# One matmul-bias-residual kernel: another order of the last loads and stores on the one DMA queue

## The chip, the cores and the metric

The kernel runs on one core of one Trainium2 chip. The metric is device time in microseconds (us), the median over several executions. Sizes in this text are binary: 1 MB is 1024 KB.

## The reference

```python
def setup_inputs():
    batch, m, k, n = 16, 512, 1024, 768
    ...

def reference(x, weight, bias, residual):
    return (np.matmul(x, weight) + bias + residual).astype(np.float32)
```

All inputs and the output are float32. x is 32 MB, the residual and the output 24 MB each, the weight 3 MB. All of it has to cross between HBM and the core once: 83 MB.

## The kernel before

**Tiling.** The 8192 rows of x are cut into eight groups of 1024 rows. Partition p of a group holds eight consecutive rows, so each partition's share of a group is one contiguous piece: 32 KB of x, 24 KB of residual, 24 KB of output. A group's x is 4 MB (`x0` to `x7`), its residual 3 MB (`r0` to `r7`), its output 3 MB (`st0` to `st7`). A letter behind the number is a part of a group: `x6a` and `x6b` are the two halves of x of group 6 (2 MB each, `PARTS`), `st7a`, `st7b` and `st7c` are three, three and two of the eight rows (`LAST_PARTS`). `st4+` is one transfer for the outputs of groups 4 and 5. `st7a` is cut further by `shares`: one transfer of partitions 16 to 127 and four of four partitions each.

**Stages.** For each half group (four row tiles of 128 rows) ScalarE casts x to bf16 (L131), VectorE transposes 32-by-32 blocks (L161 and L167), ScalarE moves blocks into place (L136), TensorE multiplies with the weight that stays in SBUF (L326), VectorE adds the residual to the product in PSUM and writes the sum over the residual in SBUF (L173), GpSimd adds the bias in place (L222, two row tiles an instruction, 32 instructions in all). The sum is then stored from the residual's place. VectorE works on half 0 of a group, then on the last four tiles of the group before it (two instructions at L173), then on half 1, then on the first four tiles of the same group. Ahead of these last it waits for the group's residual (`res.wait()` in half 1).

**Places in SBUF.** x alternates between two slots (`x_home`): group g's x can only be loaded when group g - 2 has been cast. The residuals alternate between four slots (`r_home`): the residual of group g from 4 to 6 can only be loaded when the output of group g - 4 has been stored from that slot. Group 7's residual goes into the x slot of group 6.

**Order of the transfers.** All transfers are issued by SyncE onto one DMA queue, in the order written out in `ORDER` (L17). The queue takes them one after another. In the loop at L248 SyncE meets the following waits, and a wait holds back all that is behind it in `ORDER`:

- an x of group g over 1 waits until all four casts of group g - 2 are done (L259), and until the x load before it has landed, because they count on one semaphore (`load_into`, L245, recorded at L87); the second halves (`b`) count on another;
- a residual waits until the residual before it has landed (the same L245), and in groups 4 to 6 until `st{g-4}` has landed (L274);
- the residual of group 7 waits until all casts of group 6 are done (L270); just behind that wait SyncE also releases half 1 of group 7 to ScalarE, since x7 is loaded whole (L272);
- a store waits until GpSimd has added the bias to its last tiles (L285), the last part until VectorE has written it (L283).

The lines that give the waits of the steps below:

```python
258            if g > 1 and part != "b":
259                wait(sp, "cast", 2 * (2 * g - 2))
...
269            if g == n_grp - 1:
270                wait(sp, "cast", 2 * (2 * g))
...
273            elif g > 3:
274                wait(sp, f"st{g - 4}", 16)
```

At L262 a program counts which x groups are loaded whole, so that ScalarE's wait for their second half is met.

Of the kernel before, what the change touches and what calls it, by code (L numbers as in the profile page):

```python
# [14 lines left out]
B = 4  # L15

ORDER = ("x0a bias w x0b r0 x1a x1b r1 x2 r2 x3 r3 x4 st0 "  # L17
         "st1 r4 x5 r5 st2 x6a x6b r6 x7 r7 st3 st4+ st6 st7a st7b st7c").split()
PARTS = {"": (0, 8), "a": (0, 4), "b": (4, 8)}
LAST_PARTS = {"a": (0, 3), "b": (3, 6), "c": (6, 8)}  # L20
SPLIT = "st7a"
# [342 lines left out]
```

## Time and profile before

| | us |
|---|---|
| median of 3 runs | 209.06 (208.9 to 209.13) |
| the profiled execution's own time | 209.15 |
| its span, first to last instruction | 207.4 |
| TensorE matmul busy | 170.5 (82%) |
| VectorE busy | 166.4 (80%) |
| ScalarE busy | 144.9 (70%) |
| GpSimd busy | 115.4 (56%) |
| packets on the 16 DMA engines | 98.2% of the span, 87.05 million bytes, 420 GB/s |

The span leaves out what lies before the first and behind the last instruction of the program: 209.15 - 207.4 = 1.8 us. The median, not the profiled execution, is the time that a change is compared with; the two are 0.09 us apart. A transfer has two times: its issue, when SyncE hands it to the queue, and its landing, when its semaphore is complete. The landing can be read off where SyncE waits for it: the next instruction starts some 0.05 us later.

### The profile page before, as it was taken

To read this page: it belongs to the slowest core of one execution; us is meant where nothing else is said; L and a number is where in the kernel's file an instruction comes from. 1 tells how busy PE (TensorE), PEld (TensorE's weight loads), DVE (VectorE), ACT (ScalarE), POOL (GpSimd) and SP (SyncE) were. 2 spreads that over 40 slices of the span, in tenths; PEclk is the share of its full clock that TensorE was granted. 3 is DMA by queue.
4 is the path that set the end of the run, shared out by engine and by line. 5 is a ranking of instruction groups with operands and counts; after the bars stand their busy time and mean duration, and the time that the engine had idled before them with its cause. 6 is when DMAs were issued, how large, how long until landed. Compare 5 with 4: busy or idle time off the path is not lost.

```text
span 207.4 us, 2314 instructions
## 1 busy us (share of the span) xinstructions
PE 170.5 (82%) x1024; PEld 50.6 (24%) x512; DVE 166.4 (80%) x180; ACT 144.9 (70%) x162; POOL 115.4 (56%) x38
## 2 busy tenths in 40 slices
PE   0000799999999999999999999899999999999900
PEld 0000123322222233323332333233323332222200
DVE  1185493999899998999899988998999899983510
ACT  2393966697879796979697879888797969730000
POOL 0009006609392939385856666484829391999800
PEclk9999999999999999999999999999999999999995
DMA  6999999999999999999999999999999999999995
GB/s 205 448 427 438 431 430 417 450 441 461 405 405 461 398 455 405 438 422 455 441 403 465 411 450 398 422 442 452 403 460 411 450 403 431 455 427 422 436 404 212
DMA packets 4328, 87.05 MB, mean 420 GB/s; under 512 B 484, under 2 KB 484, under 8 KB 616
## 3 DMA queue, kind: packets, MB, share of 16 engines
q1 hardware_dynamic: 4328, 87.05, 98.2%
HBM read 61.88 MB, written 25.17 MB: 420 GB/s over the span
## 4 chain that ended last, share of the span: by engine, by line
DMA 77%; PE 10%; DVE 4%; issue 2%; ACT 1%; SPq 0%; DVEq 0%; ACTq 0%
DMA data<-in_x_dram 66%; DMA out_dram<-data 12%; PE po L326 10%; DVE xt L167 2%; DVE data L173 1%; ACT xb L131 1%; DVE tq L161 1%; SPq L294 0%; DVEq L98 0%; SPq L87 0%; ACTq L98 0%; SPq L359 0%; SPq L45 0%
## 5 line engine op out<-in xcount | busy, mean ns | idle before, releaser
L326 PE MATMUL po<-w_sb,xt 128*128 128x512 bf16 (+1 forms) x1024 | 170.5, 329 | 26.1 <-issue 22.2
L222 POOL TENSOR_TENSOR data<-data,bias_bc 128x1536 f32<-128x1536 f32 x32 | 109.8, 3449 | 65.8 <-DVE data L173 65.7
L136 ACT COPY xt<-tq 32x512 uint32<-32x512 uint32 x128 | 78.9, 617 | 21.8 <-DVE tq L161 19.0
L167 DVE STREAM_TRANSPOSE xt<-xb 32x512 uint32<-32x512 uint32 x128 | 90.1, 704 | 3.9 <-ACT xb L131 2.0
L326 PEld LDWEIGHTS po<-w_sb,xt 128*128 x512 | 50.6, 99 | 145.6 <-issue 143.7
L131 ACT CAST xb<-data 128x2048 bf16 x32 | 64.8, 2076 | 15.7 <-DMA data<-in_x_dram 15.4
L173 DVE TENSOR_TENSOR data<-po,data 128x1536 f32 (+2 forms) x33 | 55.9, 1709 | 13.9 <-PE po L326 13.5
L161 DVE STREAM_TRANSPOSE tq<-xb 128x1024 uint32<-128x1024 uint32 x16 | 19.8, 1236 | 5.5 <-ACT xb L131 5.5
L217 POOL CAST w_sb<-data 128x3072 bf16<-128x3072 f32 x2 | 5.4, 2744 | 15.2 <-DMA data<-in_weight_dram 15.2
L178 DVE LOAD_MASK_SELECT bias_bc<-bias_rows x1 | 0.0, 14 | 6.6 <-DMA bias_rows<-in_bias_dram 6.6
L140 ACT ACT_TABLE_LOAD x1 | 1.3, 1283 | 1.0 <-SPq L45 1.0
L175 DVE MEMSET bias_rows<- 128x768 f32 x1 | 0.7, 698 | 1.2 <-SPq L45 1.2
L178 DVE STREAM_SHUFFLE bias_bc<-bias_rows 128x768 f32<-128x768 f32 x1 | 1.0, 1029 | 0.0
L348 POOL MEMSET const-float32-0.0<- 128x1 f32 x1 | 0.1, 99 | 0.2 <-issue 0.2
L140 ACT COPY warm<-const-float32-0.0 128x1 f32<-128x1 f32 x1 | 0.2, 191 | 0.0
L348 POOL MEMSET const-bfloat16-1.0<- 128x1 bf16 x1 | 0.1, 102 | 0.0
L348 POOL MEMSET const-uint8-127<- 128x1 uint8 x1 | 0.1, 102 | 0.0
L348 POOL MEMSET const-float32-1.0<- 128x1 f32 x1 | 0.1, 99 | 0.0
## 6 DMA issues: line engine op xcount, KB each, us to landing
data<-in_residual_dram SPq DMA_DIRECT2D x8, 3072.0 KB, 17.0
data<-in_x_dram SPq DMA_DIRECT2D x5, 4096.0 KB, 21.8
out_dram<-data SPq DMA_DIRECT2D x5, 3072.0 KB, 24.1
data<-in_x_dram SPq DMA_DIRECT2D x6, 2048.0 KB, 18.5
out_dram<-data SPq DMA_DIRECT2D x1, 6144.0 KB
data<-in_weight_dram SPq DMA_DIRECT2D x1, 3072.0 KB, 13.0
out_dram<-data SPq DMA_DIRECT2D x1, 1152.0 KB
out_dram<-data SPq DMA_DIRECT2D x1, 1008.0 KB
```

The lines of the kernel that those rows point to most:

```text
L131: act.copy(out=xb[:, c], in_=part.rearrange("p t (a j r) -> p t j a r", j=R // 2, r=2)).then_inc(sem("cast"), 1)
L136: act.copy(out=xt[q * Q:(q + 1) * Q, half, :, :, m * Q:(m + 1) * Q], in_=tq[m * Q:(m + 1) * Q, :, :, q]).then_inc(sem("mv"), 1)
L140: act.copy(out=warm[:], in_=nc.const_aps.tensor(0.0, [P, 1], FP32))
L161: dve.transpose(out=tq[:], in_=xb_words(0)).then_inc(sem("tq"), 1)
L167: ins = dve.transpose(out=xt[q * Q:(q + 1) * Q, half, :, :, m * Q:(m + 1) * Q], in_=words[m * Q:(m + 1) * Q])
L173: dve.tensor_add(out=rt, in0=po[:, j % 4:j % 4 + n, :N], in1=rt).then_inc(sem("ev"), 1)
L175: dve.memset(bias_rows[:], 0.0).then_inc(sem("ev"), EV0)
L178: dve.stream_shuffle(out=bias_bc[:], in_=bias_rows[:], mask=[0] * 32).then_inc(sem("bb"), 1)
L217: pool.tensor_copy(out=w_sb[:, part, :], in_=w_stage[:, part, :]).then_inc(sem("wc"), 1)
L222: pool.tensor_add(out=rt, in0=rt, in1=bias_bc[:, None, :].to_broadcast((P, 2, N))).then_inc(sem("add"), 1)
L326: ins = pe.add_instruction(mybir.InstMatmult(name=nc.get_next_instruction_name(), ins=[pe.lower_ap(w_sb[:, k, n0:n0 + nl]), stationary(i, k)],
L348: nc = _bacc.Bacc("TRN2", target_bir_lowering=False, num_devices=1)
```

## The change

Only the string `ORDER` is changed:

```diff
 ORDER = ("x0a bias w x0b r0 x1a x1b r1 x2 r2 x3 r3 x4 st0 "
-         "st1 r4 x5 r5 st2 x6a x6b r6 x7 r7 st3 st4+ st6 st7a st7b st7c").split()
+         "st1 r4 x5 r5 x6 st2 x7 r6 st3 r7 st4+ st6 st7a st7b st7c").split()
```

x of group 6 becomes one transfer of 4 MB in place of two of 2 MB, and stands ahead of `st2`. x of group 7 stands ahead of the residual of group 6. `st3` stands between the residuals of groups 6 and 7, no longer behind both. Through L262 group 6 now counts among the groups that are loaded whole. The instructions of all engines but SyncE are the same in number and order; SyncE issues one transfer less. The bytes are the same.

## The prediction

> **What bounds the kernel now.** I read the DMA queue's row first, then the chain of waits for the landings, then the stretches between landings, then the engines around the two groups whose transfers move.
>
> The queue's row on the page:
>
> ```profile
> q1 hardware_dynamic: 4328, 87.05, 98.2%
> ```
>
> The 16 DMA engines are occupied for 98.2% of the span. The chain of waits (start, duration, what) and, behind it, the stretches between those landings (length, busy time and instructions of each engine, clock, DMA share, GB/s):
>
> ```profile
> 54.62 17.00 DMA data<-in_x_dram
> ...
> 72.06 23.97 DMA out_dram<-data
> ...
> 96.48 24.12 DMA data<-in_x_dram
> ...
> 120.66 19.69 DMA data<-in_x_dram
> ...
> 140.41 21.87 DMA data<-in_x_dram
> ```
>
> ```profile
> 54.60:71.62 17.02, 16.53 (x102) 4.90 (x50) 16.18 (x17) 14.12 (x14) 10.86 (x4) 1.00 1.00 431
> 96.03:120.60 24.57, 24.08 (x149) 7.22 (x74) 23.59 (x26) 19.00 (x22) 13.70 (x4) 1.00 1.01 435
> 120.60:140.35 19.75, 18.75 (x116) 5.58 (x57) 18.33 (x22) 17.75 (x20) 13.73 (x4) 1.00 0.99 424
> 140.35:162.28 21.93, 21.44 (x133) 6.43 (x66) 20.98 (x23) 18.12 (x21) 13.73 (x4) 1.00 1.02 439
> 162.28:196.00 33.72, 33.23 (x205) 9.91 (x102) 27.01 (x27) 18.00 (x20) 26.68 (x8) 1.00 1.00 431
> 204.90:206.10 1.20, 0.00 (x0) 0.00 (x0) 0.00 (x0) 0.00 (x0) 0.00 (x0) 0.50 0.23 97
> ```
>
> Each piece of the chain ends with a landing: x3 at 71.62, st0 at 96.03, x5 at 120.60, x6a at 140.35, x7 at 162.28. Between them the DMA share is 0.99 to 1.02, so the reader is to see a queue that never runs dry. The pace follows: r2 and x3, 7 MB, take 17.02 us, 2.43 us a MB; x6b, r6 and x7, 9 MB, take 21.93, again 2.44. I use 2.434. At that pace the 18 MB behind x7 (r7, st3, st4+, st6, st7) would end at 162.28 + 43.81 = 206.1; SyncE's last wait, for the stores, ends at 206.5. So the kernel is a stream of 83 MB, fed without gaps from the first load to the last store. In the last 1.2 us only a quarter of the DMA time is used: the four small transfers of st7a leave four of the 16 engines with more rows, and these end last.
>
> **The change part by part.** SyncE's issues around it, before:
>
> ```profile
> 110.96 0.33 SPq L294 DMA_DIRECT2D data<-in_residual_dram  x1
> 111.34 0.42 SPq L294 DMA_DIRECT2D out_dram<-data  x1
> 120.66 0.80 SPq L294 DMA_DIRECT2D data<-in_x_dram  x2
> 135.49 0.33 SPq L294 DMA_DIRECT2D data<-in_residual_dram  x1
> 140.41 0.33 SPq L294 DMA_DIRECT2D data<-in_x_dram  x1
> 155.76 0.33 SPq L294 DMA_DIRECT2D data<-in_residual_dram  x1
> 156.14 44.00 SPq L294 DMA_DIRECT2D out_dram<-data  x10
> ```
>
> *x6 ahead of st2.* x6 still waits for x5 (120.60), so it is issued at 120.66 as now, while r5 (issued at 110.96) fills the queue until 120.60 + 3 x 2.434 = 127.9. x6 lands at 127.9 + 9.74 = 137.6; now its halves land at 140.35 and, 4.87 later, at 145.2. The wait now holds st2 back too, from 111.34 to some 121.1; no other queue is passed. st2 lands at 137.6 + 7.30 + 0.28 (priced below) = 145.2, in place of 135.5.
>
> *x7 ahead of r6.* x7 needs x6 landed (137.6) and group 5's casts (ended at 133.9), is issued at 137.7 with st2 still 7.5 us deep in the queue, and lands at 154.9 in place of 162.28. r6 needs st2's landing, is issued at 145.3 (now 135.49) behind x7's 9.7 us, and lands at 162.3 (now 152.6): up to here both orders have moved the same bytes, so this is the moment when x7 lands now.
>
> *st3 between r6 and r7.* Its bias adds ended at 117.4, so it goes out at 145.7, straight behind r6. r7 waits for group 6's casts (155.7, where half 1 of group 7 is released, as now) and for r6 (162.3). Issued there, it has st3's 7.30 us ahead of it in the queue; the first load of all took 7.33 us from issue to landing for 2 MB, so at most 7.33 - 4.87 = 2.5 us of latency, and the cover is three times that. Without st3 as cover the queue would stand for up to 2.5 us. r7 lands at 162.3 + 7.30 + 0.28 + 7.30 = 177.2 (now 169.6). st4+ needs the 24th bias add (160.9) and is held back to 162.7; its turn comes at 177.2.
>
> *Who needs the later transfers.* VectorE, ScalarE and TensorE around group 6 and 7:
>
> ```profile
> 162.56 1.76 DVE L173 TENSOR_TENSOR data<-po,data 128x1536 f32 x1
> 164.92 1.76 DVE L173 TENSOR_TENSOR data<-po,data 128x1536 f32 x1 [0.60 <-PE po L326]
> ...
> 162.40 4.07 ACT L131 CAST xb<-data 128x2048 bf16 x2 [0.42 <-DMA data<-in_x_dram]
> ...
> 175.64 20.97 PE L326 MATMUL po<-w_sb,xt 128*128 128x512 bf16 x128 [0.48 <-DVE data L173]
> 175.45 17.23 POOL L222 TENSOR_TENSOR data<-data,bias_bc 128x1536 f32<-128x1536 f32 x5 [4.19 <-DVE data L173]
> ```
>
> The add at 162.56 is the first that reads r6. Its lead shrinks from 10 us to 0.3 us. If it starts up to 0.5 us late, VectorE's 0.60 us of idle before its next add and TensorE's 0.48 us before group 7 hold it: cost nothing. Behind it wait half 0 of group 7 on VectorE, then TensorE, GpSimd and st6 and st7. r7 is first read by the third of GpSimd's five adds, at 175.45 + 2 x 3.44 = 182.3, 5 us behind its landing. ScalarE's 0.42 us for x7 vanishes, but VectorE's and TensorE's pitch of 21.46 us a group is the same in groups where no x was waited for, so this earns nothing. Stores: st6 is ready at 182.3, st7a at 192.7; the stream reaches them at 177.2 + 14.6 = 191.8 and 199.1.
>
> *Prices of the stream itself.* Bytes: the same, 0. One transfer in place of two: the stretch rich in parts, 8.29 to 32.69, moves w, x0b, r0 and x1a, 10 MB, in 24.40 us, 2.440 a MB, against 2.431 for r2 and x3: 4 x 0.009 = 0.03 us gained. A store between loads: r5, st2 and x6a, 8 MB, took 19.75 against 19.47 at the pace: 0.28 us. st1, r4, x5 took 24.57 against 24.34: 0.23, and r3, x4, st0 24.41: 0.07, so st0 and st1 together 0.30. st2 is such an island in both orders; st3 is a new one, while the turn from loads to stores at the tail stays. Its price is bounded by 0 (the landing shows the slowest DMA engine; the four that end last may not be it) and 0.30. No row says which engines lose the time, so I take the middle, 0.15. Sum: 0.15 - 0.03 = +0.12 us: 209.15 would become 209.27 against the profile's own time, and the median 209.06 becomes 209.2.
>
> The Trainium skill, DMA: Bandwidth & Descriptors, section Anatomy of one DMA, gives each transfer a fixed part of about 2.0 us besides its bytes. If that were paid in series, the merged x6 would save 2 us. The trace disagrees for a full queue: three transfers took 21.93 us where bytes alone ask 21.91.
>
> **The rivals.**
>
> *Slower: turns between loads and stores cost in full.* Each store island costs its 0.28 on the engines that end last, and the moved st2, now between two 4 MB loads, as much again as it does now, since its two neighbours run long. For it: all three stretches with such turns are over the pace. Against it: the pace is regained at once in 140.35:162.28. Price 2 x 0.28 - 0.03 = 0.53: 209.6. It decides from 0.42 us on (0.2%).
>
> *Slower: r6 comes too late.* A lateness over 0.3 + 0.5 us shifts VectorE and TensorE one to one; st7c's issue ended at 200.1 while its data are due about 204, so the end moves only from a lateness of some 3 to 4 us, a landing after 166. An island price ten times the measured one would be needed. At 7.3 us late, a whole transfer: 209.06 + about 4 = 213.
>
> *Faster: the end is the arithmetic's.* The chain of waits ends with VectorE and TensorE behind x7, and ScalarE stood 0.42 us for x7. If that shifted everything behind it, 209.06 - 0.42 = 208.6. Against it: the unbroken DMA share until 204, and the 21.46 us pitch.
>
> *Faster: fewer transfers.* By the fixed part in series, 2.0 us less. From rows: the two halves cost at most 0.03 us more than the whole; to earn 2 us, x6b would have had to land 2 us late, and 21.93 leaves 0.02.
>
> *It doesn't do what it says:* x6 keeps its issue time, 120.66. True, but the order in the queue changes regardless, so this ends in the forecast.
>
> **How the numbers follow.** Forecast, 209.2, its own range 208.9 to 209.5: 0.68. Turns in full, 209.6: 0.18. r6 late, from 209.5 up: 0.05. Arithmetic's end, 208.6: 0.07. Fewer transfers: 0.02. Within 0.2%, 0.42 us, about what a measurement of this kernel can tell from no change: 208.64 to 209.48, nearly all of the forecast, 0.66. Slower: the two slower rivals and the forecast's upper edge, 0.25. Faster: 0.09. The range 208.7 to 209.8 takes in the island's bounds and the turns in full, and leaves out r6 late and most of the faster cases.
>
> **What would show it.** In the changed profile: x loads issued at 120.7 and 137.7, r6 at 145.3, r7 at 162.3; a DMA share near 1.00 in every stretch up to 204; no ScalarE wait for x7; VectorE's first add of group 6 at 162.5 to 163.0, and group 7's matmuls still at 175.6. Wrong if a stretch's share drops below 0.97, if that add starts after 163.1, or if the span moves more than 0.4 us with these steps in place.

## The result, and the profile after

| | before | after |
|---|---|---|
| median, us | 209.07 (22 runs) | 209.50 (22 runs) |
| lowest to highest, us | 208.87 to 209.20 | 209.11 to 210.73 |
| profiled execution's own time, us | 209.15 | 209.44 |
| its span, us | 207.4 | 207.6 |

The ratio is 1.0032 with a 95% interval of 1.0021 to 1.0043: the changed kernel is slower by 0.4 us. Its runs also scatter: eight of the 22 lie from 210.06 to 210.73, a microsecond above the others, where the old kernel's lie within 0.33 us. A second series (12 runs, the last experiment below) gave 209.42 and 1.0021 (1.0011 to 1.0031).

SyncE's issues in the changed kernel (start, duration of the issue, instruction):

```profile
110.83 0.33 SPq L294 DMA_DIRECT2D data<-in_residual_dram  x1
120.54 0.33 SPq L294 DMA_DIRECT2D data<-in_x_dram  x1
120.92 0.42 SPq L294 DMA_DIRECT2D out_dram<-data  x1
137.59 0.33 SPq L294 DMA_DIRECT2D data<-in_x_dram  x1
145.15 0.33 SPq L294 DMA_DIRECT2D data<-in_residual_dram  x1
145.53 0.43 SPq L294 DMA_DIRECT2D out_dram<-data  x1
162.16 0.33 SPq L294 DMA_DIRECT2D data<-in_residual_dram  x1
162.54 0.78 SPq L294 DMA_DIRECT2D out_dram<-data  x1
```

Read from the top: r5, x6, st2, x7, r6, st3, r7, st4+, each within 0.2 us of the time forecast. The queue's row and the chain of waits (start, duration, what):

```profile
q1 hardware_dynamic: 4184, 87.05, 98.1%
```

```profile
120.54 16.98 DMA data<-in_x_dram
...
175.52 21.13 PE po L326 x128
...
196.67 0.96 DVE data L173
```

The bytes and the occupied share are the same. The last load in the chain is now x6, landing at 137.52; from there the chain goes through ScalarE, VectorE and TensorE, since no cast waits for x7 any more. The chain follows waits, and none of these waits holds the queue back, so the arithmetic is not the limit: the queue is as full as before. The engines around groups 6 and 7:

```profile
162.59 1.76 DVE L173 TENSOR_TENSOR data<-po,data 128x1536 f32 x1 [0.19 <-issue]
...
161.87 4.05 ACT L131 CAST xb<-data 128x2048 bf16 x2
...
175.52 21.12 PE L326 MATMUL po<-w_sb,xt 128*128 128x512 bf16 x128 [0.33 <-DVE data L173]
```

The first add of group 6's residual waits 0.19 us for r6 and starts at 162.59; the cast of x7 no longer waits; the last group's matmuls start at 175.52, as before (175.64). The arithmetic is where it was. What differs lies on the DMA engines, in these stretches (length, busy time of each engine, clock, DMA share, GB/s), first of the changed kernel, then of the old one:

```profile
154.82:162.14 7.32, 7.32 (x47) 2.21 (x23) 7.19 (x10) 5.92 (x10) 5.91 (x2) 1.00 1.00 430
162.14:177.15 15.01, 14.68 (x90) 4.34 (x45) 14.13 (x15) 12.79 (x12) 8.67 (x3) 1.00 0.99 424
177.15:196.00 18.85, 18.85 (x117) 5.57 (x57) 12.96 (x13) 4.94 (x8) 17.95 (x6) 1.00 1.01 435
199.50:200.50 1.00, 0.00 (x0) 0.00 (x0) 0.00 (x0) 0.00 (x0) 0.00 (x0) 1.00 0.74 295
206.10:206.50 0.40, 0.00 (x0) 0.00 (x0) 0.00 (x0) 0.00 (x0) 0.00 (x0) 0.50 0.04 15
```

```profile
199.50:200.50 1.00, 0.00 (x0) 0.00 (x0) 0.00 (x0) 0.00 (x0) 0.00 (x0) 1.00 1.02 424
206.10:206.50 0.40, 0.00 (x0) 0.00 (x0) 0.00 (x0) 0.00 (x0) 0.00 (x0) 0.50 0.00 0
```

Three things are to be seen. r6 alone, 3 MB, takes 7.32 us, the pace; st3 and r7, 6 MB, take 15.01, where the pace asks 14.60: the new turn costs 0.4 us. From 199.5 to 200.5 the DMA share is 0.74, a dry stretch that the old kernel doesn't have. And behind 206.1, when the old kernel has moved all its data, the share is 0.04, about 0.6 of one engine in sixteen.

The second and third need a finer reading. A transfer's semaphore is raised once by each DMA engine, so the trace's records of it show how far the last engine is behind the 15th:

```
landing            15th     last     lag (us)
r3    before      78.91    78.92    0.01
r4    before     110.56   110.89    0.33     behind st0 and st1
x6a   before     139.82   140.35    0.53     behind st2
r7    before     169.04   169.59    0.55
r7    after      176.31   177.15    0.84     behind st3
```

Up to the first store the last engine is 0.01 us behind the 15th in the old kernel and 0.07 in the changed one. From then on one engine lags. It is slower in the stores themselves: between 180 and 197 us, 18 of the old kernel's 300 packets of 24 KB take 0.93 to 0.95 us and all others 0.91, and 18 is one engine's share. Between loads the lag doesn't grow; at the first load behind a store it is larger than before the store. Over all fourteen profiles of this text it rose by 0.1 to 0.3 us at st2 and, where st3 stands ahead of r7, by 0.4 to 0.8 at st3; at st0 and st1 it moved by anything from -0.2 to +0.3.

The end is this engine's. In every profile the span ends 0.83 or 0.84 us behind the last landing of a store. In the old kernel five of st7c's landings come late: four from 206.13 to 206.32, the engines with three rows more of st7a, and one alone at 206.53. In the changed kernel they are 206.03 to 206.25 and 206.81. So a fifth engine ended last before the change already, and the 0.28 us by which it is later are all but 0.01 of the difference between the two profiled executions.

Two theories came out of this. Theory L: this laggard pays for the new turn, and the end is its end. Theory S: the dry stretch is the cost. SyncE took 0.8 us longer for the four small transfers of st7a than in the old kernel, and st7b, issued from 198.35 to 199.78, came when st7a had run out. Its issue in the changed kernel, then in the old one:

```profile
198.35 1.43 SPq L294 DMA_DIRECT2D out_dram<-data  x1
```

```profile
197.54 1.44 SPq L294 DMA_DIRECT2D out_dram<-data  x1
```

### The profile page after: what moved, and what is told of

The parts are those of the page before. It is cut to its first block, busy times and chain, and to the rows that moved or that the text cites. A ratio compares the mean times of both kernels' runs of the same rounds, so it can differ in the third digit from the quotient of the medians.

```text
span 207.6 us, 2313 instructions
## 1 busy us (share of the span) xinstructions
PE 170.6 (82%) x1024; PEld 50.5 (24%) x512; DVE 166.5 (80%) x180; ACT 144.9 (70%) x162; POOL 115.4 (56%) x38
## 4 chain that ended last, share of the span: by engine, by line
DMA 65%; PE 18%; DVE 7%; ACT 2%; issue 2%; SPq 0%; DVEq 0%; ACTq 0%
DMA data<-in_x_dram 54%; PE po L326 18%; DMA out_dram<-data 12%; DVE xt L167 4%; DVE data L173 2%; ACT xb L131 1%; ACT xt L136 1%; DVE tq L161 1%; SPq L294 0%; DVEq L98 0%; SPq L87 0%; ACTq L98 0%; SPq L359 0%; SPq L45 0%
```

## The experiments

Each was timed against the old kernel on the same chip; the old kernel's median was 209.00 to 209.05 in all series.

**The split of st7a taken out, in both orders.**

```diff
-SPLIT = "st7a"
+SPLIT = "none"
```

> The changed order, with st7a as one transfer in place of five. Theory T (tail): in the changed kernel SyncE hands st7b to the queue at 199.8 us, when most DMA engines have run out of st7a at 199.5, and the queue stands for some 0.3 us; the four small transfers take SyncE 5.2 us to issue. Without them st7b is issued by 197.2 at the latest, no stretch of the last 10 us before 204 falls under a DMA share of 0.95, and the time is within 0.15 us of the old order without the split (run beside it). Rival I (island): the new store between r6 and r7 costs its time on the stream itself; then this kernel is still 0.3 us or more slower than the old order without the split.

> The old order, with st7a as one transfer. It is the partner of the run before. All 16 engines then have the same rows: theory T says the last quarter-busy 1.2 us of the old kernel goes, and the time is some 0.5 to 1.2 us below the old kernel's. If the split had been needed to feed the queue, the time would be above the old kernel's.

The changed order took 209.67 us (209.31 to 210.24), 1.0033 (1.0022 to 1.0044); the old one 209.27 (209.18 to 209.46), 1.0013 (1.0004 to 1.0022). Neither has a dry stretch: st7b goes out at 196.8 and 196.5, and the DMA share is 0.93 or more in every stretch from 198 to 204.5. The changed order is still 0.40 us behind. So the difference doesn't need the dry stretch, which speaks against S and for L. The expectation that the old order would gain 0.5 to 1.2 us was wrong, and the end shows why; of the changed order without the split:

```profile
199.50:200.50 1.00, 0.00 (x0) 0.00 (x0) 0.00 (x0) 0.00 (x0) 0.00 (x0) 1.00 1.01 424
204.90:206.10 1.20, 0.00 (x0) 0.00 (x0) 0.00 (x0) 0.00 (x0) 0.00 (x0) 0.50 0.06 26
206.10:206.50 0.40, 0.00 (x0) 0.00 (x0) 0.00 (x0) 0.00 (x0) 0.00 (x0) 0.50 0.07 31
```

and of the old order without it:

```profile
199.50:200.50 1.00, 0.00 (x0) 0.00 (x0) 0.00 (x0) 0.00 (x0) 0.00 (x0) 0.67 1.01 424
204.90:206.10 1.20, 0.00 (x0) 0.00 (x0) 0.00 (x0) 0.00 (x0) 0.00 (x0) 0.50 0.06 26
206.10:206.50 0.40, 0.00 (x0) 0.00 (x0) 0.00 (x0) 0.00 (x0) 0.00 (x0) 0.50 0.00 0
```

A share of 0.06 is one engine of sixteen, alone. At the end it is 1.08 us behind the 15th in the old order and 1.84 in the changed one. The split takes a row of st7a, 0.35 us, from twelve engines, the laggard among them, and gives three rows to four others; in the old kernel these four end 0.2 us ahead of it.

**x6 merged, and nothing else.**

```diff
-         "st1 r4 x5 r5 st2 x6a x6b r6 x7 r7 st3 st4+ st6 st7a st7b st7c").split()
+         "st1 r4 x5 r5 st2 x6 r6 x7 r7 st3 st4+ st6 st7a st7b st7c").split()
```

> The old order, only x6a and x6b merged into one x6 behind st2. The queue then carries one transfer less and each DMA engine nine descriptors less, as in the changed kernel. Theory T1 (state of the queue by count): SyncE's issues in the tail slow down as in the changed kernel, st7b is issued about 199.8, time 209.4 to 209.6 with a spread of 1 us or more. Theory T2 (what stands in front of the tail): nothing changes, 209.0 to 209.1, spread under 0.4 us, st7b issued about 199.0.

210.97 us (209.17 to 211.94), 1.0084 (1.0059 to 1.0108). The question, whether a count of transfers matters, isn't answered, because the edit did something else. ScalarE in its profile:

```profile
145.14 4.06 ACT L131 CAST xb<-data 128x2048 bf16 x2 [4.76 <-DMA data<-in_x_dram]
```

With st2 ahead of it, the whole x6 lands at 145.0, 4.7 us later than x6a did. Group 6's cast waits 4.76 us, GpSimd's last adds slip, st7a is issued at 195.63 in place of 192.71, and the queue runs short from 199.5 to 201 (a DMA share of 0.75). The profiled execution took only 209.30 us, so it doesn't show where the rest of the 1.9 us lies by which the median rose. In the change x6 also moves ahead of st2 (landing at 137.5), and a run below shows that the merge is harmless there.

**x6 and x7 moved, st3 left behind r7.**

```diff
-         "st1 r4 x5 r5 st2 x6a x6b r6 x7 r7 st3 st4+ st6 st7a st7b st7c").split()
+         "st1 r4 x5 r5 x6 st2 x7 r6 r7 st3 st4+ st6 st7a st7b st7c").split()
```

> x6 whole ahead of st2 and x7 ahead of r6 as in the changed kernel, but st3 behind r7 as in the old one. Theory T2 with st3 as the cause: as the old kernel, 209.0 to 209.1, spread under 0.4 us, since the tail is again 15 MB of stores with st3 first. T1 (count): as the changed kernel, 209.4 to 209.6. Rival I: as the old kernel as well, as it has no store more between loads.

212.88 us (212.83 to 213.09), 1.019 (1.0176 to 1.0203): 3.9 us, expected by no theory. r6 is the last transfer in the queue, and r7 can only be issued when r6 has landed:

```profile
154.61:160.50 5.89, 5.89 (x38) 1.76 (x18) 5.79 (x8) 4.55 (x8) 5.89 (x2) 1.00 0.97 417
160.50:163.50 3.00, 2.95 (x19) 0.88 (x9) 2.83 (x4) 2.95 (x3) 0.05 (x1) 1.00 0.47 115
163.50:173.59 10.09, 10.04 (x62) 3.03 (x31) 9.44 (x12) 8.02 (x11) 6.86 (x2) 1.00 0.95 353
```

The queue stands around 162, then moves only 353 GB/s, and r7 lands at 173.6. By the records of the packets an engine stood 2.2 us on the mean between its last packet of r6 and its first of r7. Then 50 of r7's 128 packets of 24 KB took over 1.0 us, up to 2.2, in place of 0.91, which is 1.9 us more per engine. This is the cover that the prediction named for st3: without it the moved x loads cost 3.9 us, as the waits stand.

**The same, with r7 freed of its wait.**

```diff
-            wait(pool, "r", 16 * n_grp)
+            wait(pool, "r7", 16)
+            pool.sem_inc(sem("r"), 16)
...
-            into = load_into("r")
+            into = load_into("r" if g < n_grp - 1 else "r7")
```

> x6 whole ahead of st2 and x7 ahead of r6 as in the changed kernel, st3 behind r7 as in the old one, and r7 on a semaphore of its own, so that it is issued without waiting for r6's landing and the queue doesn't run dry (the fourth run lost 3.9 us there). If st3 between r6 and r7 is the whole cause: 209.0 to 209.15, no run above 209.4, r7's lag behind the 15th engine 0.3 to 0.6 us. If the moved x loads carry the other part (the turn at st2 between two 4 MB loads): 209.3 to 209.5, with runs above 210.

209.03 us (208.87 to 209.19), 0.9998 (0.9989 to 1.0007). The order of the run before, with r7 on a semaphore of its own, has the old kernel's time and its narrow scatter. r6 and r7:

```profile
154.94:162.24 7.30, 7.30 (x47) 2.19 (x23) 7.17 (x10) 5.90 (x10) 5.92 (x2) 1.00 1.00 431
162.24:169.55 7.31, 7.26 (x45) 2.17 (x23) 6.62 (x7) 5.38 (x5) 5.02 (x2) 1.00 1.00 430
```

So the moved and merged x loads, and st2 between two loads of 4 MB, cost nothing. What is left of the change is st3.

**st3 between the last two residuals, and nothing else.**

```diff
-         "st1 r4 x5 r5 st2 x6a x6b r6 x7 r7 st3 st4+ st6 st7a st7b st7c").split()
+         "st1 r4 x5 r5 st2 x6a x6b r6 x7 st3 r7 st4+ st6 st7a st7b st7c").split()
```

> The old order with one edit: st3 between x7 and r7, not behind r7. x6a, x6b, st2, r6 and x7 stand as before, no wait moves by more than a store, and r7 stays covered by st3. Theory L (laggard): one DMA engine lags behind the other 15; the landing of the load behind a store shows it, 0.2 to 0.3 us more at st0/st1 and at st2, 0.4 to 0.7 at st3; that engine ends last, so this edit alone costs 0.3 to 0.6 us, 209.3 to 209.6, with r7's lag behind the 15th engine about 1 us in place of 0.55. Theory S (supply: the late issue of st7b alone, for a reason in the moved x loads): no more than 0.1 us, 209.0 to 209.1.

209.15 us (208.94 to 210.46), 1.0011 (1.0000 to 1.0023). r7's lag is 1.04 us, as theory L said; the time rose by 0.1 us, less than it said, with one run of 12 at 210.46. In time theory S, which had said 0.1 us at most, is nearer. But S laid the dry stretch to the moved x loads, and here they are not moved and it is there all the same (the share is 0.61 from 199.5 to 200.5). So neither theory gives both the time and the profile of this run.

**The small transfers of st7a issued behind st7b, in the changed order.**

```diff
+        if name == SPLIT:
+            todo, held = todo[:1], todo[1:]
+        elif name == "st7b":
+            todo += held
```

> The changed order, with the four small transfers of st7a issued behind st7b and not ahead of it. st7b is then issued as soon as its bias add ends, 196.8 us, in place of 198.35 to 199.78. Theory S: no stretch before 204 runs dry, the time falls to 209.0 to 209.2 and the runs above 210 go. Theory L: the laggard still ends about 206.5, the dry stretch goes but the time stays at 209.3 to 209.6.

210.04 us (209.15 to 211.05), 1.0046 (1.0028 to 1.0065). st7b went out at 196.9, but the four small issues then took 5.3 us, and st7c, behind them, left only at 202.6:

```profile
202.50:203.50 1.00, 0.00 (x0) 0.00 (x0) 0.00 (x0) 0.00 (x0) 0.00 (x0) 0.50 0.34 138
204.90:206.10 1.20, 0.00 (x0) 0.00 (x0) 0.00 (x0) 0.00 (x0) 0.00 (x0) 0.50 0.55 220
206.10:207.40 1.30, 0.00 (x0) 0.00 (x0) 0.00 (x0) 0.00 (x0) 0.00 (x0) 0.50 0.07 28
```

The dry stretch only moved, to 203, so this doesn't separate the theories. Its profiled execution took 210.56 us, and shows such a run: one engine alone from 206.1 to 207.4. Its lag at st4+, 1.28 us, is no larger than in the first profile of the changed kernel (1.26). From its landing of st6 to its last one it took 8.26 us, against 7.07 in the old kernel, and seven packets of 9216 bytes took over 0.4 us, up to 0.93, where the old kernel has none. So 1.2 us were lost behind st6, in the stretch of the slow packets, and not at the turn at st3.

**st7a on 15 engines, in both orders.**

```diff
-    return [slice(APART, P)] + [slice(m, APART, STEP) for m in range(STEP)]
+    return [slice(0, 120), slice(120, P)]
```

> The old order; st7a is cut into partitions 0 to 119 and 120 to 127 in place of one large and four small transfers. If the large one runs on 15 engines with eight rows each and leaves out the last engine, and the last engine is the laggard, its 2.8 us of st7a are taken from it, all others get at most one row of 0.35 us more, and the time falls below the old kernel's by 0.8 to 1.3 us (207.8 to 208.3), with no quarter-busy stretch at the end. If the laggard is another engine, it gets a row more: 209.2 to 209.6.

> The changed order with st7a cut as in the run before. Theory L, if the last engine is the laggard: what the turn at st3 costs falls on an engine that now has 2.8 us of slack, so this comes out within 0.2 us of the old order cut the same way. If st3's turn costs all engines, or if the laggard is another engine, it stays 0.3 us or more above it.

212.90 us (210.53 to 213.15), 1.0147 (1.0107 to 1.0187), and 213.38 (213.28 to 213.53), 1.0209 (1.0195 to 1.0222). Neither answers the question: in each, 57 of the 256 packets of 9216 bytes took over 0.4 us, up to 1.16 and 1.92, where the old kernel's take 0.35 to 0.39. Whether the last engine is the laggard isn't told, and the 0.5 us between the two says little beside a scatter of 2.6.

**Two small transfers of eight partitions in place of four of four, in both orders.**

```diff
-APART, STEP = 16, 4
+APART, STEP = 16, 2
```

> The old order, with the 16 partitions that st7a leaves out sent as two transfers of eight partitions in place of four of four. If these run on eight engines, each gets 9 rows of st7a (two more than the others) in place of 11 on four engines: the last quarter-busy stretch of 1.2 us shrinks to 0.7 us with half the engines, and SyncE issues two transfers less, so st7b goes out by 197.5. Time 208.4 to 208.9, unless the lagging engine is one of the eight; then 209.2 to 209.6.

> The changed order with the same two transfers of eight partitions. Theory S: st7b is issued by 197.5, the dry stretch is gone, and the time is within 0.15 us of the run before this one. Theory L: the dry stretch is gone, but the one lagging engine still sets the end; 0.3 us or more above the run before this one, with runs above it by 1 us.

209.66 us (209.51 to 209.86), 1.0028 (1.0018 to 1.0039), and 211.83 (209.78 to 212.84), 1.0112 (1.0065 to 1.0158). st7b is issued at 196.6 and 196.7, the share stays at 0.93 or more from 198 to 203.5, and the changed order is 2.2 us behind the old one. At the end of the changed order:

```profile
204.90:206.10 1.20, 0.00 (x0) 0.00 (x0) 0.00 (x0) 0.00 (x0) 0.00 (x0) 0.50 0.15 64
206.10:208.50 2.40, 0.00 (x0) 0.00 (x0) 0.00 (x0) 0.00 (x0) 0.00 (x0) 0.50 0.06 26
```

One engine runs on alone for 2.4 us. The dry stretch is gone and the difference is not, but most of it is something else than the turn at st3: ten packets of 9216 bytes took over 0.4 us, up to 1.28 (two in the old order's run, up to 0.98). The last engine's landing of st6 is 0.4 us later than in the old order (199.78 against 199.36), its last landing 2.0 us later (209.08 against 207.05), so 1.6 us came behind st6. The two fastest of the six runs, 209.78 and 209.91, are only 0.1 and 0.3 us above the old order's median. So this pair can't size the turn.

The old order's run tells where the laggard is. Eight engines land st7c from 204.63 to 204.92, seven from 205.2 to 205.8, one at 207.05. The laggard is not among the eight without added rows, so it is one of the eight whose load the edit raises, by two rows of 0.35 us; that is about what the old order lost (0.6 us).

**The changed kernel once more.**

> The changed kernel once more, for its spread beside the other runs of this call: 209.4 to 209.6 in the middle, about a third of the runs from 210.0 to 210.7. If the profiled execution is one of these, it shows whether one DMA engine runs on alone for more than 0.6 us at the end (theory L) or the dry stretch at 199.5 to 200.3 is longer than in the first profile (theory S).

209.42 us (209.06 to 210.24), two of 12 runs above 210, 1.0021 (1.0011 to 1.0031). The profiled execution took 209.26 us:

```profile
199.50:200.50 1.00, 0.00 (x0) 0.00 (x0) 0.00 (x0) 0.00 (x0) 0.00 (x0) 0.70 0.32 129
206.10:206.50 0.40, 0.00 (x0) 0.00 (x0) 0.00 (x0) 0.00 (x0) 0.00 (x0) 0.50 0.00 0
```

Here the queue is much drier than in the first profile (0.32 against 0.74), and yet the run is 0.2 us shorter (209.44), and nothing is moved behind 206.1. A share of 0.32 is five engines. The four with three rows more and the laggard would be five; the engines that stand end well ahead of them, at 205.8 against 206.64, and have time to spare.

**All profiles together.** The lag of the last engine at two landings that every kernel has; kernels in which the queue ran dry or late before the tail are left out:

```
                                    r7     st4+ (us)
st3 behind r7     before           0.55    1.22
                  x moved, r7 free 0.44    1.12
                  no split         0.15    0.85
                  two small        0.52    1.21
                  15 engines       0.55    1.23
st3 ahead of r7   after            0.84    1.26
                  after again      1.03    1.44
                  st3 only         1.04    1.51
                  small late       0.86    1.28
                  no split         1.25    1.66
                  two small        1.31    1.74
                  15 engines       1.04    1.48
```

The two groups don't overlap in either column. At st4+ all have moved the same bytes; the means are 1.13 and 1.48 us, 0.35 apart. The nearest two are 0.03 apart, and the first profiles of the old and the changed kernel 0.04, so a single pair of profiles shows little.

The packets show where the 0.35 us arise. In each of the seven profiles with st3 ahead of r7, one packet of r7, at 174.5 to 174.8 us, takes 0.27 to 0.68 us longer than the usual 0.91 for 24 KB (with slower ones beside it in the run with 15 engines). In none of the other five is there one. Taken off, the lags at st4+ would be 0.8 to 1.2 us, as in the first group, so this packet is nearly all of what the turn costs. st3 had landed by 169.8, five microseconds earlier. What makes the packet slow is not shown.

The last engine's landings show what becomes of it:

```
                                   st4+      st6      last (us)
st3 behind r7   before            192.06   199.46   206.53
                x moved, r7 free  192.03   199.47   206.51
                no split          191.78   199.22   206.57
                two small         191.90   199.36   207.05
st3 ahead of r7 after             192.13   199.56   206.81
                after again       192.18   199.59   206.64
                st3 only          192.24   199.65   206.70
                small late        192.25   199.65   207.91
                no split          192.39   199.84   207.17
                two small         192.34   199.78   209.08
```

Without the split, where no packet of 9216 bytes took over 0.4 us, the changed order is 0.61 us later at st4+ and 0.60 at the end: the lag is carried through unchanged. With the split the three profiles of the changed kernel and of st3 alone are later by 0.07 to 0.18 us at st4+ and by 0.11 to 0.28 at the end; in the first of them 0.2 us came behind st6, where two packets of 9216 bytes took 0.66 and 0.73 us. So two things make the last engine late: what the turn at st3 brings, and slow packets of the last stores.

## Why the prediction was right in its range and wrong in its size

*The bound and the schedule: right.* Every issue and landing came within 0.2 us of the forecast; r6 came 0.19 us late for VectorE and nothing behind it moved, TensorE's pitch included. "r6 too late" and "the end is the arithmetic's" fall: x7 landed 7.5 us earlier and the end did not.

*The moved x loads at nothing: right.* The run with r7 freed has the ratio 0.9998 (0.9989 to 1.0007). In "turns in full" the part that charged st2 a second time falls with it.

*The merge at -0.03 us: not told apart from 0.* Merging alone raised the median by 1.9 us, with x6a's early landing lost, which the prediction didn't need because x6 moves ahead of st2.

*The cover for r7: right, with a part of its price left out.* It said that without st3 the queue would stand for up to 2.5 us; the engines stood 2.2 us. The run without it lost 3.9 us, because r7's packets were slow after the stand, 1.9 us per engine. Nothing in the prediction allowed for that.

*The new turn at 0.15 us: this is the term that failed.* Its bounds were 0 and 0.30, and the middle was taken because "No row says which engines lose the time". It is one engine, and this engine ended last in the old kernel already. The prediction read that the four engines with more rows of st7a "end last"; the landings show a fifth behind them (206.53 against 206.32). So the bound of 0 was not open, and the turn's price had to be charged in full. The lag that it adds is 0.35 us at st4+ on the mean of all profiles. The median rose by 0.43 and 0.38 us, and without the split by 0.40; with st3 alone it rose by 0.10 only. The rows for the right choice were there: each landing read off the chain is the landing of the slowest engine, and the 0.28 us at st2 were never made up again on the way to x7. The rival "turns in full" gave the sign and nearly the time (209.6); half of its price was for st2, which costs nothing more, so its own turn was undersized as well. The measured 209.50 lies in the range because the range was drawn to take that rival in; the forecast's own sum, +0.12 us, is not what happened. The chance of 0.66 for no change was too high for a kernel whose tail had been left with no slack on its slowest engine.

*Not foreseen: the dry stretch.* The prediction looked at when the stream reaches st7a and st7c, and not at st7b behind the four small issues, where the old kernel had about 0.7 us to spare (issue ended at 198.98, st7a ran out at about 199.7). The pair without the split has the same difference without it, so it is not the cost there; but "a DMA share near 1.00 in every stretch up to 204" was wrong, and the sign that the prediction set for itself, a share below 0.97, came true.

*The fixed part of a DMA.* That three transfers took 21.93 us where bytes alone ask 21.91 proves less than the prediction says, since the pace was taken in part from these three. The stretch with more transfers tells more: 2.440 us a MB with four, 2.431 with two. The Trainium skill, DMA: Bandwidth & Descriptors, section Anatomy of one DMA, is about DMAs issued from GpSimd, and puts most of the fixed 2 us of one into the receipt of the last write. All loads and stores here are issued from SyncE, and the run without st3 shows the parts for r6 and r7: 0.5 us from the end of r6's last packet (161.44) to its landing (161.92), and 1.0 us from r7's issue (161.93) to its first packet (162.89). So here the receipt is not the larger part. Where the queue is full the runs show nothing of either.

*Open.* There is no profile of one of the changed kernel's own runs above 210 us. The two profiles of such runs in related kernels (small transfers late, two small) lost 1.2 and 1.6 us behind st6, with seven and ten slow packets, so slow packets of the last stores are a likelier cause of the others than a larger lag at the turn. What makes packets slow is not shown, neither these nor the one in r7. st3 alone cost 0.1 us and the whole change 0.4 (0.2 to 0.4 in two series) while the x moves alone cost nothing; the intervals touch (1.0023 against 1.0011 and 1.0021), and what joins to them, if anything, is not settled. Why SyncE's small issues took 4.4 us in the old kernel, 5.2 in the changed one and 2.5 where the queue was 4 us behind is not known. No version beat the old kernel.

## What to carry to other kernels

In this unbroken stream of transfers the order of equal bytes was nearly free, apart from one place where a load followed a store. So count such places, and charge each to the slowest DMA engine, not to the mean: the landing of a transfer is that engine's landing. Before moving a store out from between two loads, or into it, look which wait the load behind it has: a load that waits for the landing of the transfer just ahead needs something else in the queue. And read the last microseconds by the single engines: a DMA share of 0.06 is one engine of 16, and a tail that is cut to fit one engine's lag loses when that lag grows.

## What the runs showed of the hardware

- One of the 16 DMA engines is slower in stores: 0.93 to 0.95 us for a packet of 24 KB against 0.91 (18 of 300 packets, 180 to 197 us, old kernel). Its lag is 0.6 us or less up to the last load ahead of st3, and up to 1.8 us at the end where all engines have the same rows. The Trainium skill, DMA: Bandwidth & Descriptors, section Latency and other measured facts, says that engines 7 and 15 are usually slower, and guesses that the software descriptor rings are behind it. Here one engine lags while its transfers are on the one hardware queue of SyncE, so that guess can't be the whole cause of this lag. The trace doesn't number the engines, so whether it is engine 7 or 15 is not shown.
- With a store between the last two residuals, one packet of the second residual took 0.27 to 0.68 us more than the usual 0.91, five microseconds behind the store's landing, in seven profiles of seven; in the five with the store behind both there is none.
- A store's issue of four partitions took 0.6 to 2.1 us of SyncE, against 0.33 to 0.43 for most issues of 128 partitions.
- With a transfer of 120 partitions and one of eight in place of st7a, 57 of 256 packets of 9216 bytes took between 0.4 and 1.9 us, against 0.35.
- A queue that had run dry once cost 3.9 us: 2.2 us of standing and then packets of up to 2.2 us in place of 0.91, with 353 GB/s over the 10 us up to r7's landing.
